# High and low parts of the attention's q and k split at the projection, not at each head's operands

## The chip, the cores and the metric

One core of a Trainium2 chip runs the kernel. The metric is the device time of one execution in microseconds, as the median of several runs. The core has five engines that work side by side, each taking its own queue of instructions in order: TensorE (PE, with its weight loads as PEld), VectorE (DVE), ScalarE (ACT), GpSimd (POOL) and SyncE (SP), which here issues every transfer (DMA).

## The reference

One decoder layer over 2048 tokens of width 1024, in float32. The embedding is normalised and modulated by a vector c; one projection `h @ w_in` gives two groups of eight heads of 64 channels each and a gate. Group A is a recurrence (RWKV-7); group B is causal attention with a bias from running forget gates:

```
proj = h @ w_in                                   # (2048, 4232)
q_f, k_f, v_f = ...                               # three slices of 512 columns, 8 heads of 64
logit[t, s] = q_t . k_s / 8 + cum[t] - cum[s]     # cum: running sum of log sigmoid of the forget gate
y_b = softmax over s <= t of logit, times v
y = concat(y_a, y_b) * silu(gate part of proj)
out = LayerNorm(alpha * x + (1 + gate_c) * (y @ w_out))
```

## The kernel before

The tokens are worked on in two halves of 1024, each in two blocks of 512. For each half there is a stretch of the recurrence and then a stretch of attention; the projection's matmuls fill TensorE beside them, ahead of need, and the output projection with the final norm ends the kernel. All work is written as generators (streams). A driver (lines 138 to 284) keeps a model of each engine's time and emits the instruction whose stream comes first by that model, so the order in each engine's queue follows from modelled costs and from when buffers come free in the model. A program change in one stream can therefore move the instructions of others.

The large products are made in the format float32r. To keep precision the kernel splits a factor x: its high part is what a copy into that format leaves of it, its low part is x minus the high part. A product is then high times high, high times low and low times high.

The steps that the change touches:

- `ev_fox` (982 to 995) takes a 128x512 tile of q, k, v or gate (two heads, 512 tokens) out of PSUM into a part of the tile `arena` (18 parts of 128x512, handed out by `slots`), stores it in DRAM (`fscr`, seen in the profile as kscr, qscr, vscr and gscr), and gives the PSUM bank back. There are 16 such tiles of q and 16 of k.
- `fox_ops` (1553 to 1582) makes four kinds of operands for each head and 512 tokens, each in a part of the tile `fx_s` (21 parts). k1 holds the high part of k in 64 rows, and three rows below: ones, and the forget sums in two parts. q1 holds the high part of q, and three rows: minus the row maximum, and two rows of ones (the first row is 0 until the maximum is known). k2 holds high k above low k, q2 low q above high q. For each, `conv` loads the raw 64x512 from DRAM into a part of `arena` (`fox_load`), ACT copies it into the operand (rounding to the high part), and for k2 POOL, for q2 DVE, subtracts that from the raw value into the other 64 rows. The three rows of k1 come by a small load from `cscr`; those of q1 are copied by DVE from the column `qrow`. Half 0 needs 64 operands (4 kinds, 2 blocks, 8 heads), half 1 needs 96, since its queries see the keys of both halves.
- `fox_guard` (1586 to 1648) multiplies q1 and k1, takes each query's largest score with DVE, and stores minus that maximum into the first of q1's three rows by a transfer (`fx_s<-mrow`). `fox_s` (1709 to 1739) waits for it, then takes for each 128 keys k1 by q1 plus k2 by q2, of which ACT makes exponentials.

In attention of half 1 DVE also prepares the output weights (`final_w`) and the rows for the final norm; those are not changed. All instructions go through one helper, so the profile gives line 134 for nearly all of them, and one has to go by tiles: `fx_s` are the attention's operands, `fx_p` its exponentials, `fx_v` its values, `rw_s` the recurrence, `ps` PSUM, `wsp` the split weights of the projection.

Of the kernel before, what the change touches and what calls it, by code (L numbers as in the profile page):

```python
# [9 lines left out]
F32 = mybir.dt.float32  # L10
# [3 lines left out]
OP = mybir.AluOpType  # L14
# [12 lines left out]
class Slots:  # L27
    """Equal parts of one tile; a part is handed out when its last use lies in the past."""
# [5 lines left out]
    def find(self, n):  # L34
        """The parts that are free first; a single one rather beside one in use, two rather at an even place."""
        best = None
        for i in self.free_:
            if all(i + j in self.free_ for j in range(n)):
                a = max(self.free_[i + j] for j in range(n))
                k = (max(a, self.drv.now), (i ^ 1) in self.free_ if n == 1 else i % 2, a)  # L40
                if best is None or k < best[0]:
                    best = (k, a, i)
        return best and best[1:]
# [20 lines left out]
class Slot:  # L64
# [14 lines left out]
    def drop(self):  # L79
        """Gives back the first part only."""  # L80
# [35 lines left out]
class Engine:  # L116
    """An engine whose instructions are also timed by the driver's model."""
# [20 lines left out]
class Driver:  # L138
    """Orders the emission. Every stream is a generator that emits a step and goes on when a model of the engines
    says that the step has ended. It yields 0 to wait for another stream, ("at", ns) to wait for a time, "pe" to  # L140
    go on as soon as the tensor engine has nothing else to do."""
# [91 lines left out]
    @contextmanager  # L233
    def side(self):
        """What is emitted here doesn't hold up its stream."""
        self.count = False
        yield
        self.count = True
# [50 lines left out]
def hymba_kernel(ctx: ExitStack, tc, x, c, emb_ln_g, emb_ln_b, w_ada, b_ada, w_in, rwkv_mix, w0,  # L289
# [50 lines left out]
    fscr = [{k: [dram.tile([128, TB], F32, name=f"{k}scr{h}{i}") for i in range(4)] for k in "qkvg"} for h in range(2)]  # L340
# [30 lines left out]
    qrow = const.tile([128, 1], F32, name="qrow")  # L371
# [48 lines left out]
    def start_loads():  # L420
        """In the order in which they are needed; the short ones between the long ones."""
# [43 lines left out]
    def start_ada(kt):  # L465
        """Shift and scale of 128 channels: four parts of the sum side by side, added up as they are transposed."""
# [30 lines left out]
    def start_lora():  # L497
        """Both low-rank factors in two parts: 0 and 1 the high part twice, 2 the low parts."""
# [22 lines left out]
    def warm():  # L521
        """Keeps the tensor engine's clock up until there is work for it."""
# [6 lines left out]
    def start_consts():  # L529
        """derived columns of pc: 0-12 one minus mix; 13-16 half a0; 17-20 half w0; 21-24 one minus k_a;  # L530
        25-32 scale, 33-40 shift of the modulated embedding"""
# [50 lines left out]
        pool.memset(qrow, 1.0)  # L582
        pool.memset(qrow[64:65], 0.0)
# [35 lines left out]
    def rsqrt(o, u, n):  # L619
        """o = u ** -0.5 on [128, n], one Newton step after the power."""  # L620
# [20 lines left out]
    def ln_group(i, xs, left):  # L641
        """Normalises some tiles of x: mean and 1/sqrt(var + eps) stay in stats."""
# [70 lines left out]
    def ln_early(b, blk, kt):  # L713
        """The first half: transposed before the factors of the modulation are known."""
# [60 lines left out]
    def plan():  # L775
        """The next 128 columns of the input projection, or tokens of the output projection."""
# [23 lines left out]
    class EarlyW:  # L800
        """More room for the first of them."""
# [7 lines left out]
    def weights():  # L809
        """Loads what the tensor engine's wide products take as the stationary operand, and splits it in two."""  # L810
# [47 lines left out]
    def proj_stream():  # L858
        """The first tiles of all go side by side, block by block; so do the last two of a half."""
# [32 lines left out]
    def shift_mix(b, g, o):  # L892
        """o = proj * (1 - mix) + previous token's proj * mix, along the free axis."""
# [17 lines left out]
    def ev_f(b, half, blk):  # L911
        """Forget gates, heads on partitions: rows of ones, and of the running sum of -8 log f in two parts."""
# [49 lines left out]
    def silu(b, g):  # L962
        """Twice the SiLU of a bank."""
# [18 lines left out]
    def ev_fox(k):  # L982
        def ev(b, half, p, blk):
            s = yield from slots.get(1)
            if k == "g":
                yield from silu(b, s)
            else:
# [3 lines left out]
            sp.dma_start(fscr[half][k][p][:, blk * NB:(blk + 1) * NB], s.ap)  # L991
# [36 lines left out]
    def bcast_rows(b, r8, w):  # L1028
        """[128 tokens, 4 tiles, n heads] -> [(head, 64 channels), 512 tokens] in a bank."""
# [7 lines left out]
    def head_sums(b, sq):  # L1037
        """Four tiles side by side, each sum 16 times, turned to [128 tokens, (4 tiles, 2 heads, 16)] in columns 128-255."""
# [13 lines left out]
    def rwkv_elem(half, p, blk, dl, u):  # L1052
        """The factors of the recurrence, decays folded in: u.kr = (kk, r), u.bk = (b, k) or (k, b) by chunk."""
# [114 lines left out]
    def rwkv_scores(u):  # L1168
        """Masked products of every chunk, the transposed factors and the right side of the solve.
        u.am: against kk; u.zs: against r, beside the transposed (b, k); u.rh: (kk, products times v) by head."""  # L1170
# [77 lines left out]
    def rwkv_solve(n, u, qt):  # L1248
        """(I + A)^-1, transposed, of every chunk and head: the two diagonal blocks, then the block between them.
        A block's rows go to 4 partitions of its quadrant, 8 rows each, beside the whole block of A."""  # L1250
# [168 lines left out]
    def rwkv_low(half, blk):  # L1419
        """Both low-rank inputs in two parts, one above the other."""  # L1420
# [28 lines left out]
    def rwkv_stream(half):  # L1449
        """All pairs of heads, both 512-token blocks of the half: unit n = 2 * pair + block."""  # L1450
# [102 lines left out]
    def fox_ops(half, st):  # L1553
        """Operands of every head: k1 = [high k; 1; -8 cum in two parts], k2 = [high k; low k],
        q1 = [high q; -row maximum; 1; 1], q2 = [low q; high q]; the maximum is 0 while it is looked for."""
        def conv(key, o, H, name, b4):
            h = H % 2
            while (b4 // 2, H // 2, name[0] + "f", b4 % 2) not in res:
                yield 0
            at = hs(1) if name == "q2" else hs(0)  # L1560
            s = yield from fox_load(name[0], H // 2, hs(h), b4 * NB, at)
            if name == "k1":
                c = (b4 % 2) * NB
                sp.dma_start(o.f[64:67], cscr[b4 // 2][:, H, c:c + NB])
            yield
            act.activation(o.ap[at], s.ap[at], AF.Copy)
            if name == "q1":
                dve.tensor_copy(o.ap[64:67], qrow[64:67, 0:1].to_broadcast([3, 512]))
            yield
            if name[1] == "2":  # L1570
                to = hs(0) if name == "q2" else hs(1)
                tt(o.ap[to], s.ap[at], o.f[at], OP.subtract, pool if name == "k2" else dve)
                yield
            s.free()
# [11 lines left out]
    def fox_guard(half, st):  # L1586
        """The row maxima of every block of queries."""
# [64 lines left out]
    def fox_exp(b, P, n0, diag):  # L1652
        """What lies after the query gets 0 once its exponential is there, whatever that is."""
# [371 lines left out]
```

## Time and profile before

| what | us |
|---|---|
| median of 3 runs | 1948.76 |
| lowest and highest run | 1947.16, 1949.63 |
| span of the profiled execution | 1952.8 |
| PE busy in it | 1805.3 (92%) |
| DVE busy | 1522.0 (78%) |
| ACT busy | 865.2 (44%) |
| POOL busy | 853.8 (44%) |

The profiled execution is one more execution, recorded by the hardware profiler; its span runs from its first to its last instruction, and no other time of it is known. "Busy" is the share of the span in which an engine executes. Matmuls are pipelined and their ends are modelled, so that a busy PE need not be PE at its peak.

### The profile page before, as it was taken

How to read it: one execution, taken by the hardware profiler on the slowest of the kernel's cores; microseconds unless marked ns; L12 is line 12 of the kernel's file. 1: busy time of each engine (PE TensorE's matmuls, PEld its weight loads, DVE VectorE, ACT ScalarE, POOL GpSimd, SP SyncE). 2: the span in 40 equal slices, each digit the busy share in tenths (PEclk: the TensorE clock that was granted, in tenths of full speed). 3: DMA queues.
4: the chain of work that ended last, by engine and by line, in shares of the span. 5: the costliest groups of instructions: out<-in, count | busy, mean ns of one | idle time of the engine just before them, and what ended most of it. 6: DMA issues, size and time to landing. Idle time of an engine off the chain costs nothing.

```text
span 1952.8 us, 31040 instructions
## 1 busy us (share of the span) xinstructions
PE 1805.3 (92%) x11049; PEld 1289.4 (66%) x11049; DVE 1522.0 (78%) x3638; ACT 865.2 (44%) x1667; POOL 853.8 (44%) x821
## 2 busy tenths in 40 slices
PE   8999989989899999999898989988999999999997
PEld 6767666767677556677676667666755554547876
DVE  5887797778863986777876887776387789887998
ACT  3464344534444665554453433533445565642000
POOL 2232341423323576733332432232247776776653
PEclk9999899999999999999998999988999999999999
DMA  9231110111113633221111111021372233213442
GB/s 286 71 104 39 49 53 23 45 47 39 55 49 114 181 113 120 81 85 57 33 58 34 49 53 39 27 60 51 111 240 69 69 97 97 88 57 103 141 134 103
DMA packets 160909, 162.24 MB, mean 83 GB/s; under 512 B 10289, under 2 KB 114306, under 8 KB 160754
## 3 DMA queue, kind: packets, MB, share of 16 engines
q1 hardware_dynamic: 160754, 160.25, 27.2%
q8 instruction: 88, 1.44, 0.3%
q14 instruction: 67, 0.55, 0.1%
HBM read 121.41 MB, written 38.73 MB: 82 GB/s over the span
## 4 chain that ended last, share of the span: by engine, by line
PE 43%; DVE 38%; issue 5%; ACT 5%; POOL 4%; DMA 3%; SPq 1%; POOLq 0%; DVEq 0%; ACTq 0%
PE ps L134 43%; DVE rw_s L134 18%; DVE arena L134 6%; DVE small L134 5%; ACT rw_s L134 4%; DVE end_s L134 2%; DVE fx_p L134 2%; DVE state L134 1%; DVE fx_s L134 1%; POOL wsp L134 1%; DVE ps L134 1%; SPq L134 1%; POOL fx_p L134 1%; DMA ada_t<-in_w_ada_dram 1%; DMA arena<-vscr 1%
## 5 line engine op out<-in xcount | busy, mean ns | idle before, releaser
L134 PE MATMUL ps<-ht,wsp 128*128 128x512 f32 x3840 | 1003.3, 408 | 6.5 <-POOL wsp L134 5.5
L134 PEld LDWEIGHTS ps<-ht,wsp 128*128 128x128 f32 x3840 | 717.2, 194 | 166.5 <-issue 9.7
L134 DVE TENSOR_TENSOR rw_s<-rw_s 128x60 f32<-128x60 f32 (+24 forms) x1056 | 338.1, 324 | 43.4 <-ACT rw_s L134 16.2
L134 POOL TENSOR_TENSOR wsp<-wst,wsp 128x1024 fp32r<-128x1024 f32 x79 | 193.9, 2455 | 267.4 <-ACT wsp L134 234.0
L134 ACT ACTIVATE rw_s<-ps 64x256 f32<-64x256 f32 (+3 forms) x448 | 179.4, 416 | 277.8 <-PE ps L134 166.5
L134 PE MATMUL ps<-rw_s 32*32 32x32 f32 (+3 forms) x2816 | 210.7, 257 | 61.9 <-DVE rw_s L134 56.4
L134 PE MATMUL ps<-fx_s 67*128 67x512 f32 (+6 forms) x960 | 259.6, 388 | 7.8 <-DVE small L134 6.5
L134 PEld LDWEIGHTS ps<-rw_s 32*32 32x32 f32 (+3 forms) x2816 | 183.5, 165 | 104.2 <-issue 47.2
L134 PEld LDWEIGHTS ps<-fx_s 67*128 67x128 f32 (+1 forms) x960 | 163.6, 191 | 124.0 <-issue 51.7
L134 ACT ACTIVATE fx_p<-ps 128x512 f32<-128x512 f32 (+3 forms) x336 | 161.6, 518 | 149.4 <-PE ps L134 126.2
L134 POOL TENSOR_TENSOR fx_p<-fx_p 128x512 f32<-128x512 f32 (+2 forms) x160 | 188.0, 1181 | 80.3 <-PE ps L134 72.6
L134 POOL TENSOR_TENSOR small<-small,nhalf 128x8 f32<-128x8 f32 (+1 forms) x48 | 71.8, 1500 | 284.9 <-DVE small L134 205.8
L134 PE MATMUL ps<-fx_p,fx_v 128*64 128x512 f32 (+3 forms) x640 | 158.7, 554 | 1.8 <-POOL fx_p L134 1.8
L134 DVE TENSOR_REDUCE small<-ps 128x1 f32<-128x512 f32 (+1 forms) x208 | 134.6, 680 | 25.0 <-PE ps L134 24.4
L134 DVE TENSOR_TENSOR fx_p<-fx_p 128x512 f32<-128x512 f32 (+1 forms) x128 | 116.2, 908 | 43.0 <-POOL fx_p L134 40.4
L134 ACT ACTIVATE wsp<-wst 128x1024 fp32r<-128x1024 f32 x80 | 84.3, 1053 | 135.3 <-DMA wst<-yscr 101.7
L134 ACT ACTIVATE arena<-ps 128x512 f32<-128x512 f32 (+2 forms) x130 | 74.8, 578 | 148.4 <-PE ps L134 143.1
L134 POOL TENSOR_TENSOR rw_s<-rw_s,arena 128x512 f32<-128x512 f32 x64 | 83.9, 1314 | 126.5 <-ACT arena L134 74.6
L134 ACT ACTIVATE fx_s<-arena 64x512 fp32r<-64x512 f32 x160 | 96.3, 624 | 13.1 <-DMA arena<-qscr 7.7
L134 DVE TENSOR_SCALAR state<-ps,dl 64x64 f32<-64x64 f32 x256 | 72.3, 282 | 29.2 <-PE ps L134 23.1
L134 DVE STREAM_TRANSPOSE rw_s<-rw_s 32x256 f32<-32x256 f32 (+1 forms) x112 | 61.7, 551 | 40.9 <-ACT rw_s L134 38.3
L134 ACT ACTIVATE rw_s<-rw_s 32x256 f32<-32x256 f32 (+1 forms) x144 | 83.3, 600 | 16.6 <-DVE rw_s L134 15.2
(151 smaller groups left out, 2067.7 us busy)
## 6 DMA issues: line engine op xcount, KB each, us to landing
wst<-in_w_in_dram SPq DMA_DIRECT2D x66, 512.0 KB
arena<-kscr SPq DMA_DIRECT2D x96, 128.0 KB
ada_t<-in_w_ada_dram SPq DMA_DIRECT2D x16, 512.0 KB
rw_l<-lowscr SPq DMA_DIRECT2D x32, 256.0 KB
arena<-qscr SPq DMA_DIRECT2D x64, 128.0 KB
arena<-in_x_dram SPq DMA_DIRECT2D x16, 512.0 KB
wst<-yscr SPq DMA_DIRECT2D x16, 512.0 KB
xe<-in_x_dram SPq DMA_DIRECT2D x8, 512.0 KB
```

The costliest lines, as they stand in the source:

```text
L134: return fn(*args, **kw)
```

## The change

DRAM keeps two tiles for each tile of q and k, its two parts, in the order in which the second operand wants them: high above low for k, low above high for q. `ev_fox` makes both: the ACT copy out of PSUM rounds to the high part, and DVE subtracts it from the PSUM bank for the low part; each is stored by a transfer of its own. `conv` in `fox_ops` then only issues transfers into the operand: two of 64 rows for k2 and q2, one of 64 rows and one of three rows for k1 and q1. The three rows of q1 (0, 1, 1) are stored in DRAM (`qscr1`) once at the start. The copies, subtractions and the staging in `arena` fall away, and `qrow` with them. Texts that only describe functions are also taken out.

```
-    fscr = [{k: [dram.tile([128, TB], F32, name=f"{k}scr{h}{i}") for i in range(4)] for k in "qkvg"} for h in range(2)]
+    fscr = [{k: [dram.tile([2, 128, TB] if k in "qk" else [128, TB], F32, name=f"{k}scr{h}{i}") for i in range(4)]
+             for k in "qkvg"} for h in range(2)]
+    qscr1 = dram.tile([3, 512], F32, name="qscr1")
...
-        pool.memset(qrow, 1.0)
-        pool.memset(qrow[64:65], 0.0)
+        qr = yield from slots.get()
+        pool.memset(qr.ap[0:3], 1.0)
+        pool.memset(qr.ap[0:1], 0.0)
+        sp.dma_start(qscr1, qr.ap[0:3])
+        qr.free()
...
     def ev_fox(k):
         def ev(b, half, p, blk):
             s = yield from slots.get(1)
+            to = fscr[half][k][p]
+            cols = slice(blk * NB, (blk + 1) * NB)
             if k == "g":
                 yield from silu(b, s)
-            else:
+            elif k == "v":
                 act.activation(s.ap, b.ap, AF.Copy)
                 b.free()
                 yield
-            sp.dma_start(fscr[half][k][p][:, blk * NB:(blk + 1) * NB], s.ap)
+            else:
+                l = yield from slots.get(1)
+                act.activation(s.r, b.ap, AF.Copy)
+                yield
+                tt(l.r, b.ap, s.ap, OP.subtract)
+                b.free()
+                i = int(k == "q")
+                sp.dma_start(to[i, :, cols], s.ap)
+                yield
+                sp.dma_start(to[1 - i, :, cols], l.ap)
+                l.free()
+            if k in "vg":
+                sp.dma_start(to[:, cols], s.ap)
             s.free()
             yield
             res[half, p, k + "f", blk] = True
...
         def conv(key, o, H, name, b4):
-            h = H % 2
             while (b4 // 2, H // 2, name[0] + "f", b4 % 2) not in res:
                 yield 0
-            at = hs(1) if name == "q2" else hs(0)
-            s = yield from fox_load(name[0], H // 2, hs(h), b4 * NB, at)
-            if name == "k1":
-                c = (b4 % 2) * NB
-                sp.dma_start(o.f[64:67], cscr[b4 // 2][:, H, c:c + NB])
-            yield
-            act.activation(o.ap[at], s.ap[at], AF.Copy)
-            if name == "q1":
-                dve.tensor_copy(o.ap[64:67], qrow[64:67, 0:1].to_broadcast([3, 512]))
-            yield
+            src = fscr[b4 // 2][name[0]][H // 2]
+            c = (b4 % 2) * NB
             if name[1] == "2":
-                to = hs(0) if name == "q2" else hs(1)
-                tt(o.ap[to], s.ap[at], o.f[at], OP.subtract, pool if name == "k2" else dve)
-                yield
-            s.free()
+                for i in range(2):
+                    sp.dma_start(o.f[hs(i)], src[i, hs(H % 2), c:c + NB])
+            else:
+                sp.dma_start(o.f[0:64], src[int(name == "q1"), hs(H % 2), c:c + NB])
+                sp.dma_start(o.f[64:67], cscr[b4 // 2][:, H, c:c + NB] if name == "k1" else qscr1)
+            yield
             st["ops"][key] = o
```

## Rows read from the trace of the kernel before

**Rows 1.** Busy us (count) by stage: PE, PEld, DVE, ACT, POOL; clock, DMA, GB/s.
```profile
130.00:615.00 485.00, 444.43 (x3312) 339.34 (x3312) 371.74 (x1117) 212.12 (x422) 156.13 (x162) 0.94 0.16 47
615.00:835.00 220.00, 210.40 (x1134) 137.88 (x1133) 168.47 (x347) 133.82 (x271) 146.99 (x168) 1.00 0.43 131
835.00:1395.00 560.00, 504.69 (x3565) 388.03 (x3565) 411.94 (x1175) 239.94 (x462) 174.25 (x171) 0.93 0.17 49
1395.00:1780.00 385.00, 373.40 (x1684) 209.76 (x1682) 310.80 (x519) 205.74 (x410) 254.83 (x237) 0.99 0.34 104
1780.00:1952.80 172.80, 157.20 (x683) 128.40 (x682) 160.16 (x237) 13.82 (x13) 87.77 (x44) 0.97 0.38 128
```

**Rows 2.** Chain of waits by line: 130-615, 640-835, 835-1395, 1425-1600, 1600-1780 us.
```profile
by line: PE ps L134 40.8%; DVE rw_s L134 34.1%; ACT rw_s L134 8.7%; DVE arena L134 4.3%; issue 3.6%; DVE small L134 3.0%; DVE state L134 2.6%; POOL small L134 1.2%; ACT arena L134 0.5%; POOL wsp L134 0.5%; POOL rw_s L134 0.4%; DVE car L134 
...
by line: PE ps L134 55.3%; DVE small L134 7.3%; POOL fx_p L134 5.8%; DVE ps L134 5.2%; DVE fx_s L134 4.3%; DVE fx_p L134 4.3%; issue 3.7%; DVE arena L134 3.6%; POOL wsp L134 2.4%; DMA arena<-vscr 2.1%; ACT arena L134 1.7%; ACT ht L134 1.0%;
...
by line: PE ps L134 44.5%; DVE rw_s L134 33.3%; ACT rw_s L134 5.1%; DVE arena L134 4.8%; issue 4.3%; DVE small L134 3.4%; DVE state L134 2.0%; ACT arena L134 0.7%; POOL rw_s L134 0.5%; POOL wsp L134 0.4%; DVE car L134 0.3%; POOL rw_l L134 0
...
by line: PE ps L134 94.7%; DVE small L134 1.1%; issue 1.1%; POOL fx_s L134 1.0%; DVE fx_p L134 0.9%; DVE fx_s L134 0.4%; DVE arena L134 0.4%; ACT fx_p L134 0.3%; POOL fx_p L134 0.2%; POOLq L134 0.0%
...
by line: PE ps L134 31.0%; DVE small L134 16.2%; DVE fx_p L134 12.2%; issue 10.0%; DVE arena L134 7.9%; DVE fx_s L134 5.6%; DVE ps L134 4.8%; POOL fx_p L134 3.7%; DVE ht L134 3.5%; POOL arena L134 2.0%; DMA arena<-kscr 1.3%; POOL fx_s L134 
```

**Rows 3.** Groups by shape, whole trace: busy us, mean ns, idle before.
```profile
L134 ACT ACTIVATE fx_s<-arena 64x512 fp32r<-64x512 f32 x160 | 96.3, 624 | 13.1 <-DMA arena<-qscr 7.7 <-DMA arena<-kscr 3.9
...
L134 DVE TENSOR_TENSOR fx_p<-fx_p 128x512 f32<-128x512 f32 x96 | 94.1, 980 | 40.9 <-POOL fx_p L134 38.8 <-ACT fx_p L134 1.1
...
L134 POOL TENSOR_TENSOR fx_s<-arena,fx_s 64x512 fp32r<-64x512 f32 x48 | 70.9, 1486 | 23.5 <-ACT fx_s L134 18.2 <-issue 2.0 <-POOL fx_p L134 1.1
...
L134 DVE TENSOR_TENSOR fx_s<-arena,fx_s 64x512 fp32r<-64x512 f32 x32 | 31.5, 994 | 0.7
...
L134 DVE CAST fx_s<-qrow 3x512 fp32r<-3x512 f32 x32 | 28.8, 916 | 0.7
...
L134 DVE TENSOR_TENSOR arena<-ps,arena 128x512 f32<-128x512 f32 x32 | 21.8, 682 | 1.0 <-PE ps L134 0.7
```

**Rows 4.** Busy time by stretch, instructions on tile fx_s alone; columns as rows 1.
```profile
615.00:835.00 220.00, 70.89 (x288) 47.91 (x288) 27.29 (x32) 38.47 (x64) 24.26 (x16) 1.00 0.43 131
1395.00:1600.00 205.00, 100.15 (x365) 62.74 (x365) 19.41 (x20) 36.31 (x61) 28.38 (x19) 1.00 0.40 124
1600.00:1780.00 180.00, 88.58 (x309) 52.94 (x307) 13.59 (x12) 21.47 (x36) 18.28 (x13) 0.98 0.27 81
```

**Rows 5.** Busy time of the late part of attention 1; columns as rows 1.
```profile
1600.00:1780.00 180.00, 171.88 (x768) 91.39 (x766) 156.81 (x249) 93.65 (x185) 132.27 (x121) 0.98 0.27 81
```

**Rows 6.** Issues on SyncE's queue, ns min/median/max: whole; recurrence 0; recurrence 1.
```profile
L134 SPq DMA_DIRECT2D arena<-kscr x96: 444/458/1427, 621.6 to 1722.9; - x96
L134 SPq DMA_DIRECT2D kscr<-arena x16: 320/332/383, 118.9 to 1423.7; - x16
...
L134 SPq DMA_DIRECT2D qscr<-arena x6: 319/324/345, 141.6 to 603.2; - x6
...
L134 SPq DMA_DIRECT2D kscr<-arena x6: 320/329/383, 902.7 to 1348.1; - x6
```

**Rows 7.** Timeline from 1614 us, VectorE and GpSimd: start, length.
```profile
1614.17 0.67 DVE L134 TENSOR_TENSOR fx_p<-fx_p 128x512 f32<-128x512 f32 x1
...
1614.85 1.27 POOL L134 TENSOR_TENSOR fx_s<-arena,fx_s 64x512 fp32r<-64x512 f32 x1 [1.01 <-issue]
1614.88 1.79 DVE L134 TENSOR_TENSOR fx_s<-arena,fx_s 64x512 fp32r<-64x512 f32 x1
```

**Rows 8.** Costliest groups of the page, GpSimd.
```profile
L134 POOL TENSOR_TENSOR fx_p<-fx_p 128x512 f32<-128x512 f32 (+2 forms) x160 | 188.0, 1181 | 80.3 <-PE ps L134 72.6
```

**Rows 9.** Waits of SyncE's queue in attention 1: us, times, longest.
```profile
SPq L134 <- ACT mrow L134: 42.3, 11, 11.6
...
SPq L134 <- PE ps L134: 12.7, 13, 2.8
```

More of the change, by code (lines that the diff above doesn't have):

```diff
@@ L370, in hymba_kernel @@
     wf = const.tile([128, KT, 8], F32, name="wf")
-    qrow = const.tile([128, 1], F32, name="qrow")
     state = const.tile([128, 2, 4, 2, 64], F32, name="state")
@@ L1556, in conv @@
         def conv(key, o, H, name, b4):
-            h = H % 2
             while (b4 // 2, H // 2, name[0] + "f", b4 % 2) not in res:
                 yield 0
-            at = hs(1) if name == "q2" else hs(0)
-            s = yield from fox_load(name[0], H // 2, hs(h), b4 * NB, at)
-            if name == "k1":
-                c = (b4 % 2) * NB
-                sp.dma_start(o.f[64:67], cscr[b4 // 2][:, H, c:c + NB])
-            yield
-            act.activation(o.ap[at], s.ap[at], AF.Copy)
-            if name == "q1":
-                dve.tensor_copy(o.ap[64:67], qrow[64:67, 0:1].to_broadcast([3, 512]))
-            yield
-            if name[1] == "2":
-                to = hs(0) if name == "q2" else hs(1)
-                tt(o.ap[to], s.ap[at], o.f[at], OP.subtract, pool if name == "k2" else dve)
-                yield
-            s.free()
+            src = fscr[b4 // 2][name[0]][H // 2]
+            c = (b4 % 2) * NB
+            if name[1] == "2":
+                for i in range(2):
[3 more added lines that the diff above has]
+                sp.dma_start(o.f[64:67], cscr[b4 // 2][:, H, c:c + NB] if name == "k1" else qscr1)
+            yield
             st["ops"][key] = o
```

## The prediction

> **What bounds the kernel now.** An average over unlike stages decides nothing, so I first cut the span where the work changes, with the view of busy time by stretch [rows 1]: recurrence of half 0 (130 to 615 us), attention of half 0 (615 to 835), recurrence of half 1 (835 to 1395), attention of half 1 (1395 to 1780) and the tail. TensorE (PE) is 90 to 92% busy in the recurrences and 96 to 97% in the attention stages; VectorE (DVE) is at 74 to 81%, and at 93% in the tail. ScalarE (ACT) and GpSimd (POOL), from which the change takes most work, are at 53 to 67% even in the attention stages.
>
> Then I read the chain of waits stage by stage, to see which engine sets the end [rows 2]. In the recurrences it is 41 to 45% PE and 44% DVE (its lines rw_s, arena, small and state added up). In attention 0 it is 55% PE and 25% DVE. Attention 1 has two regimes: until 1600 us 95% PE, from then on only 31% PE and some 50% DVE. ACT has no line over 2% in any attention stretch. So what the change takes from ACT buys almost nothing by itself, and what it does to DVE counts in every stretch but one.
>
> **What it removes.** 160 ACT copies into the operands (96.3 us), 48 POOL subtractions for k2 (70.9), 32 DVE subtractions for q2 (31.5) and 32 DVE copies of three constant rows (28.8) [rows 3]. All lie in the attention stages; the DVE part is 27.3 us in attention 0, 19.4 until 1600 and 13.6 from 1600 to 1780 [rows 4].
>
> How much of that lies on the path? The chain's line "DVE fx_s" is just these two DVE instructions.
> - 1600 to 1780: 5.6% of 180 us [rows 2], 10.1 us of the 13.6 busy. The bounds are 0 and 13.6; I take 10, since DVE leads the chain there.
> - 1425 to 1600: DVE fx_s 0.4% and POOL fx_s 1.0% of 175 us [rows 2], 2.5 us. The bounds are 0 and 19.4; I take 2.5, since PE holds 95% of the chain.
> - 640 to 835: 4.3% of 195 us [rows 2], 8.4 us. But PE idles only 220.0 - 210.4 = 9.6 us in that stage [rows 1], and the projection matmuls that fill it must be done some time anyway. The bounds are 0 and 9.6; I take 7.
>
> Gains: 10 + 2.5 + 7 = 19.5 us.
>
> PE's busy share needs a second look, for 171.9 us busy of 180 would leave only 8 to gain after 1600. The weight loads fill 91 us of those 180, against 339 of 485 in recurrence 0 [rows 1, 5]. Per microsecond PE gets less done there than elsewhere although it is "busy": its matmuls stand waiting inside their recorded times. So the chain is my measure, and 10 us may pass the 8.
> *The Trainium skill (Perfetto Trace Analysis, Identifying the Most-Contended Engine) says that matmul busy time is no measure of headroom and that the busy share of the weight loads is. By the first the late stretch could give 8 us, by the second all 13.6 of its DVE time. The trace agrees with the second, in that the two shares part ways where the chain leaves PE.*
>
> **What it adds.** Each of the 32 tiles of q and k that leave the projection takes one more DVE subtraction, 128x512, one input in PSUM. The nearest row has the same shape and kinds of operands: 682 ns [rows 3], so 21.8 us of DVE in all. By the stores to DRAM, ten of the 32 fall into recurrence 0 and twelve into recurrence 1 [rows 6] (the rows show the six of q in recurrence 0, beside which there are four of k, and the six of k in recurrence 1, beside six of q), two come before 130 us and eight in the attention stages. An instruction put into DVE's queue costs as much as DVE's time is on the path there. In recurrence 0, DVE has 44.0% of the chain and is busy 371.7 of 485.0 us, 76.6% [rows 1, 2], so 57%; in recurrence 1 it is 43.5% against 73.6%, 59%. Hence 10 x 0.682 x 0.57 = 3.9 and 12 x 0.682 x 0.59 = 4.8 us. The two early ones add 1. For the eight in attention, 24.7% against 76.6% makes 32%: 8 x 0.682 x 0.32 = 1.8. Costs: 11.5 us; bounds 0 (all in DVE's gaps) and 21.8 (all on the path).
>
> **What it moves.** The ACT copy out of PSUM stays, and only rounds its output. The bank goes back after the subtraction, 0.68 us and a hand-over later. With eight banks I put that at 0; if PE stood for the bank each time it would be 32 x 0.68 = 22 us. A second part of the arena is held meanwhile, while 160 short holdings of it go: 0. The row of constants is stored once, beside the start's transfers; under 1 us if not hidden.
>
> Transfers: 160 loads of 128 KB and 48 of 6 KB become 240 and 80, and 32 stores come on top. A load takes 0.45 us of SP's queue, a store 0.33 [rows 6]: in attention 0, 16 rows of constants and 32 second halves are 48 issues, 22 us; in attention 1, 16 and 48 are 64, 29 us. The DMA engines are 43% and 34% busy there [rows 1]; that is no limit. What counts is the order. SP takes its queue in turn, and a load now goes straight into the operand's tile: SP itself waits for the last matmul that read the tile, where before the load went to the arena and the ACT copy did that waiting. Behind it stand the stores of the row maxima, which fox_s waits for, and the weight loads. Against that, an operand needs no copy (0.62 us) and no subtraction (0.99 or 1.49 us at the mean [rows 3]) after it has landed. I put the two together at 0; the price if the queue binds is the third rival's.
>
> **Sum.** -19.5 + 11.5 = -8 us. The profiled span is 1952.8 us, and the median of the runs, 1948.8, lies 4 below it; a term of 8 us is the same against either. So 1948.8 - 8 = 1941 us.
>
> **The rivals.**
> 1. *More: POOL lets go of DVE.* A q2 subtraction took 1.79 us while POOL's k2 subtraction ran beside it; a sum of two SBUF tiles, twice as many partitions and the same length, had taken DVE 0.67 just before, alone [rows 7]. Those sums have a mean of 980 ns over 96 [rows 3]: 96 x (0.98 - 0.67) = 30 us of stretch. POOL's two-input work in attention is 188.0 us on fx_p [rows 8] and 70.9 on fx_s; without the latter, 27%, about 8 us of stretch should go. With all the DVE time after 1600 (13.6 instead of 10) and half the costs: 19.5 + 3.6 + 8 - 6 = 25 us less, 1924. Against it: part of the stretch lies before 1600, where PE leads. *The Trainium skill (SBUF — State Buffer, Who interferes with whom) has POOL and DVE share a pair of ports that one instruction locks whole when DVE reads two tiles of SBUF; with one input in PSUM DVE doesn't contend. The trace agrees with the first half: 1.79 against 0.67 us. By that rule the added subtractions stay at 682 ns.*
> 2. *No change.* PE's work is untouched. If PE's busy share binds after all, the attention stages give back a third of the 9.6 and 8.1 us that PE idles, 6 us, and half of the costs takes it away: 1949.
> 3. *Slower: SP's queue binds in attention 1.* SP waits there 42.3 us for the row maxima and 12.7 for PE [rows 9]. The 12.7 stand beside 32 loads of constants that go straight into operands; with all 96 operands loaded so they would be 38, 25 more. With the 29 us of issues SP's queue grows by 54 us. Much of it can replace waits for work that isn't due. If half lies ahead of a row maximum or an operand that PE then wants, 27 us: 1941 + 27 = 1968. It makes the kernel slower than before from 8 of the 54 us on. Against it: SP is seldom named in the chain in the attention stretches, and an operand is asked for a head ahead.
>
> **How the numbers follow.** Forecast (1933 to 1945): 0.42. Rival 1 (1915 to 1933): 0.19. Rival 2 (1945 to 1953): 0.18. Rival 3 (1953 to 1968): 0.21. A change under 0.2%, 4 us, is about what a measurement of this kernel can't tell. So faster is 0.61, same 0.18, slower 0.21. The likeliest case's own range is 1933 to 1945. The range for 8 in 10 must reach into both signs: 1920 leaves out the far end of rival 1 and 1959 that of rival 3, one in ten each.
>
> **What would show it.** Right: no ACT, POOL or DVE instruction writes fx_s any more; DVE's busy time falls by some 38 us (60.3 less 21.8), ACT's by 96, POOL's by 71; attention 1 is some 12 us shorter, attention 0 some 5 to 7, each recurrence 4 to 5 longer. For rival 1, DVE's mean for sums of fx_p falls well below 980 ns. For rival 3, SP's waits for PE in attention 1 pass 38 us, and PE waits for loads of fx_s. What would make it wrong in either direction: the order of all instructions is written by a model of the engines, which now sees other costs, so any stage may be reordered by several microseconds for reasons in none of these terms.

## The result and the profile after

The changed kernel takes 1915.32 us (median of 4 runs, 1910.95 to 1920.98) against 1947.96 for the kernel before beside it (4 runs). The ratio is 0.9831, with a 95% interval of 0.9803 to 0.9859: 33 us faster, where 8 were forecast and 1920 to 1959 was the range. The profiled execution fell from a span of 1952.8 us to 1912.4.

The page of the changed kernel: the engines' busy time, and the chain that ended last by engine.
```profile
span 1912.4 us, 30878 instructions
...
PE 1786.4 (93%) x11049; PEld 1278.3 (67%) x11049; DVE 1474.0 (77%) x3606; ACT 781.2 (41%) x1507; POOL 777.3 (41%) x773
...
PE 45%; DVE 37%; ACT 6%; issue 4%; DMA 4%; POOL 3%; SPq 2%; POOLq 0%; DVEq 0%; ACTq 0%
```
Against the table of before, ACT has lost 84 us of busy time, POOL 76.5 and DVE 48. That is mostly the work that the change takes out, and PE has the same 11049 matmuls.

Groups by shape, to be read beside [rows 3]: busy us, mean ns of one, idle before.
```profile
L134 DVE TENSOR_TENSOR fx_p<-fx_p 128x512 f32<-128x512 f32 x96 | 87.3, 909 | 58.0 <-POOL fx_p L134 57.5
...
L134 DVE TENSOR_TENSOR arena<-ps,arena 128x512 fp32r<-128x512 f32 x32 | 22.0, 686 | 38.5 <-ACT arena L134 38.3
```
The added subtraction costs 686 ns, as its neighbour in [rows 3] did (682). The sums of fx_p fell from 980 to 909 ns.

The stages, cut where [rows 1] cut them, at the last store of each half's recurrence or attention: recurrence 0, attention 0, the norm and recurrence 1, attention 1, tail.
```profile
131.00:619.00 488.00, 450.48 (x3376) 345.37 (x3377) 378.60 (x1130) 216.34 (x428) 158.28 (x162) 0.97 0.18 55
619.00:814.00 195.00, 192.46 (x1060) 123.75 (x1059) 139.00 (x312) 93.33 (x199) 112.54 (x146) 1.00 0.54 165
814.00:1363.00 549.00, 507.14 (x3627) 390.42 (x3626) 419.59 (x1196) 246.00 (x469) 176.92 (x176) 0.97 0.20 59
1363.00:1739.00 376.00, 361.63 (x1627) 202.07 (x1626) 274.48 (x480) 152.64 (x312) 208.31 (x205) 0.97 0.39 123
1739.00:1912.40 173.40, 159.55 (x700) 130.81 (x698) 160.95 (x246) 13.84 (x13) 85.90 (x43) 0.98 0.39 132
```
The clock column stands out: 0.97 in both recurrences, where [rows 1] have 0.94 and 0.93. The trace holds each stretch in which TensorE was granted half speed (1.2 instead of 2.4 GHz). Half of their length is a first estimate of what they cost. With the projection's matmuls (128x512, 0.256 us of PE's time each: 981.3 us by 3840) counted in every stage, the two profiles compare so:

| stage | us before, after | lost at half speed | projection matmuls |
|---|---|---|---|
| start | 128.1, 131.4 | 5.1, 3.4 | 201, 207 |
| recurrence 0 | 488.2, 487.2 | 27.3, 17.1 | 1053, 1091 |
| attention 0 | 214.0, 195.7 | 0, 0 | 313, 269 |
| norm of half 1 | 48.0, 53.6 | 0, 0 | 179, 212 |
| recurrence 1 | 518.0, 494.6 | 39.3, 17.1 | 1107, 1106 |
| attention 1 | 386.6, 376.1 | 3.4, 10.2 | 320, 255 |
| tail | 169.9, 173.8 | 4.5, 3.8 | 667, 700 |

Of the 40.4 us between the two profiles, 28.0 are half speed. Without it and with every projection matmul charged where it runs, the rest is -12.4 us: attention and norm -10.6, recurrences -1.4, start +3.5, tail -3.8. In what follows, "full-clock time" is the span times the mean granted clock, taken for every run: 1873.5 us before (median of 73 runs) and 1859.3 after. It treats the whole span as if it went by TensorE's clock. Among those 73 runs 0.010 of clock goes with 15.6 us where the product counts 20, so it makes the clock's share somewhat too large.

### The profile page after: what moved, and what is told of

The parts are those of the page before. It is cut to its first block, busy times and chain, and to the rows that moved or that the text cites. A ratio compares the mean times of both kernels' runs of the same rounds, so it can differ in the third digit from the quotient of the medians.

```text
span 1912.4 us, 30878 instructions
## 1 busy us (share of the span) xinstructions
PE 1786.4 (93%) x11049; PEld 1278.3 (67%) x11049; DVE 1474.0 (77%) x3606; ACT 781.2 (41%) x1507; POOL 777.3 (41%) x773
## 4 chain that ended last, share of the span: by engine, by line
PE 45%; DVE 37%; ACT 6%; issue 4%; DMA 4%; POOL 3%; SPq 2%; POOLq 0%; DVEq 0%; ACTq 0%
PE ps L134 45%; DVE rw_s L134 19%; DVE arena L134 8%; ACT rw_s L134 4%; DVE small L134 4%; DVE end_s L134 3%; SPq L134 2%; DVE state L134 2%; DVE fx_p L134 1%; DMA wst<-in_w_in_dram 1%; DVE ht L134 1%; POOL wsp L134 1%; ACT arena L134 1%; POOL small L134 1%; DMA arena<-vscr 1%
## 5 line engine op out<-in xcount | busy, mean ns | idle before, releaser
L134 PE MATMUL ps<-ht,wsp 128*128 128x512 f32 x3840 | 981.3, 403 | 4.2 <-POOL wsp L134 3.5
L134 PEld LDWEIGHTS ps<-ht,wsp 128*128 128x128 f32 x3840 | 707.5, 191 | 161.0 <-issue 10.0
L134 ACT ACTIVATE rw_s<-ps 64x256 f32<-64x256 f32 (+2 forms) x448 | 181.7, 418 | 264.4 <-PE ps L134 134.0
L134 PE MATMUL ps<-fx_s 67*128 67x512 f32 (+5 forms) x960 | 257.5, 390 | 4.4 <-ACT mrow L134 2.3
L134 PEld LDWEIGHTS ps<-rw_s 32*32 32x32 f32 (+3 forms) x2816 | 179.4, 161 | 95.5 <-issue 55.9
L134 DVE TENSOR_TENSOR fx_p<-fx_p 128x512 f32<-128x512 f32 (+1 forms) x128 | 111.5, 871 | 64.1 <-POOL fx_p L134 62.2
L134 ACT ACTIVATE arena<-ps 128x512 f32<-128x512 f32 (+3 forms) x130 | 75.0, 579 | 174.1 <-PE ps L134 169.8
L134 ACT ACTIVATE wsp<-wst 128x1024 fp32r<-128x1024 f32 x80 | 84.2, 1053 | 143.0 <-PE ps L134 69.6
L134 DVE TENSOR_TENSOR arena<-ps,arena 128x512 fp32r<-128x512 f32 (+4 forms) x108 | 73.2, 678 | 43.7 <-ACT arena L134 40.7
L134 ACT ACTIVATE rw_s<-rw_s 32x256 f32<-32x256 f32 (+1 forms) x144 | 83.4, 601 | 19.2 <-DVE rw_s L134 17.7
```

The source lines that it names most:

```text
L134: return fn(*args, **kw)
```

## The experiments

The theories after the result were these. *Work*: the gain is the removed work, in the attention stages. *Order*: the gain comes from the new order of all instructions, which the kernel's model of the engines writes out anew when any cost changes, and through it from TensorE's clock. What each expects is in the words recorded before every run.

### Old order with the light work, new order with the heavy work

e1 keeps the order of before on every engine. The 160 ACT copies, 80 subtractions and 32 constant rows are counted in the order but not issued; transfers go straight into the operands. The low parts are zero and q and k stay whole at the projection.
```
-            act.activation(o.ap[at], s.ap[at], AF.Copy)
+            drv.time(act, "activation", [o.ap[at], s.ap[at]], {})
```


> The kernel before with its order of instructions on every engine, but the heads' copies and subtractions are left out and transfers go straight into the operands (the low parts are zeros, so the output lacks them; the split at the projection is not made). Theory A (the work taken off the engines acts where it lay, whatever the order): about 1948 - 20 = 1928, attention 0 some 7 to 12 us shorter, attention 1 some 12, recurrence 1 unchanged. Theory B (the rewritten order and the faster clock that goes with it carry most): 1940 to 1948.

e2 keeps the changed kernel's order and adds stand-ins for all the removed work, written into unused rows of the operands and unknown to the model.
```
+            nc.scalar.activation(dst, src_, AF.Copy)
+            if name == "q1":
+                nc.vector.tensor_copy(t.ap[96:99], nhalf[96:99, 0:1].to_broadcast([3, 512]))
+            if name == "q2":
+                nc.vector.tensor_tensor(dst, src_, src_, op=OP.subtract)
+            if name == "k2":
+                nc.gpsimd.tensor_tensor(dst, src_, src_, op=OP.subtract)
```


> The changed kernel with its order, and beside it dummies of the removed work at the same points: 160 ACT copies, 32 DVE subtractions and 32 DVE row copies, 48 POOL subtractions, which nothing waits for. Theory A: it gives back about 20 us or more, 1935 to 1942, all of it in the attention stages. Theory B: it gives back under 10 us, 1915 to 1925, and recurrence 1 stays at 495 us.

Measured: e1 1945.06 us, ratio 0.9987 (0.9952 to 1.0021); e2 2001.28, 1.0272 (1.0203 to 1.034). At full clock e1 is 1861, 12 less than before, and its clock is 0.958 against 0.963, so that nearly all of it is lost again. The 12 us lie in the attention stages (-4 and -8 by the reckoning of the table above), and half speed takes 11.8 us more in the profile (91.4 for 79.6). In time e1 came out as theory B had it. e2 misses both figures, and goes theory A's way much further than A had it: work that the order does not know costs 31 us in attention 0 and 57 in attention 1, of which 12 and 27 are half speed by the same first estimate. Recurrence 1, which holds none of the removed work, is the clean part. Busy time in it, for before, after, e1 and e2 (columns as [rows 1]):
```profile
878.30:1396.30 518.00, 466.36 (x3390) 357.92 (x3391) 379.60 (x1118) 216.53 (x428) 159.98 (x163) 0.92 0.16 47
```
```profile
867.90:1362.50 494.60, 454.39 (x3390) 348.57 (x3390) 383.28 (x1131) 217.54 (x429) 159.84 (x163) 0.97 0.18 54
```
```profile
879.90:1403.70 523.80, 470.23 (x3390) 360.64 (x3391) 381.61 (x1118) 216.87 (x428) 160.26 (x163) 0.92 0.16 46
```
```profile
900.80:1398.40 497.60, 458.53 (x3390) 351.63 (x3390) 380.19 (x1131) 217.25 (x429) 159.62 (x163) 0.96 0.18 53
```
All four do the same 3390 matmuls. The length goes with the order (518 and 524, 495 and 498), not with the work. So the 23 us of recurrence 1 are the order's, and 22 of them are half speed (39.3 less 17.1).

### The added subtractions alone

e3 is the kernel before, with its order, plus the 32 VectorE subtractions behind the projection and 32 more stores, all unknown to the model.
```
                 act.activation(s.ap, b.ap, AF.Copy)
+                if k in "qk":
+                    nc.vector.tensor_tensor(b.ap, b.ap, s.ap, op=OP.subtract)
+                    nc.sync.dma_start(xscr, s.ap)
                 b.free()
```


> The kernel before in its order, with the 32 added DVE subtractions (into the bank itself, result unused) and 32 added stores where q and k leave the projection. The forecast's cost: 11.5 us, 1959, with 4 to 5 us in each recurrence. If DVE's gaps hide them: 1948 to 1951.

Measured 1976.46 us, ratio 1.0161 (1.0099 to 1.0223), at full clock 17 us more, and over both figures. But not where the prediction has it: recurrence 0 is 7 us shorter and recurrence 1 7 us longer, while attention 1, with four of the 32, is 20 us longer (386.6 to 407.1). In recurrence 0 and attention 1 most of this is the clock: with half speed taken off, recurrence 0 changes by +0.1, recurrence 1 by +5.1 and attention 1 by +3.2. The extra stores lie in the same places, so this run doesn't tell the two apart.

### The same kernels in other orders

One constant of the model is changed and nothing else: ACT's latency from 165 to 180 ns (e4 on before, e5 on after), the cost of an issue on SP from 600 to 640 (e7, e6), DVE's latency from 130 to 145 (e11, e8), PE's from 197 to 212 (e14, e15). As an example:
```
-LATENCY = dict(pe=197.0, act=165.0, dve=130.0, pool=100.0, sp=0.0)
+LATENCY = dict(pe=197.0, act=180.0, dve=130.0, pool=100.0, sp=0.0)
```


> The kernel before, only the model's latency of ACT set from 165 to 180 ns: the same work in another order. Theory A: within 0.3% of before (1942 to 1954). Theory B, where the order alone moves the time by about a per cent: anything between 1925 and 1970, and the recurrences change by 10 us or more at equal counts of PE instructions, with the granted clock moving along.

> The changed kernel, the model's latency of ACT set from 165 to 180 ns, as in the earlier run of the kernel before that came to 1970. If the change is worth some 33 us whatever the order, about 1970 - 33 = 1937. If its order was a lucky draw and the change itself is worth the forecast's 8 us, about 1962. Recurrence 1 back at 505 to 520 us with a granted clock of 0.92 to 0.94 would say that its 23 us are the order's.

> The changed kernel, the model's cost of an issue on SP set from 600 to 640 ns. Same reading against its pair, the kernel before with the same model: 33 us apart if the change is worth that in any order, 8 if only the forecast's, with the sign open if luck decides.

> The kernel before, the model's cost of an issue on SP set from 600 to 640 ns: the pair of the run above. By luck of the order alone 1935 to 1975.

> The changed kernel, the model's latency of DVE set from 130 to 145 ns. A third draw of the order: within 10 us of 1915 if the order counts little once the work is gone, 1925 to 1950 if 1915 was a good draw.

> The kernel before, its order written with the model's latency of VectorE at 145 instead of 130 ns: the partner of the changed kernel under the same model (1956). Theory A (the change is worth 12 to 15 us of full-clock time in any order, and the clock is the order's): full-clock time 1870 to 1882 against 1862; the time itself 1945 to 1985, on either side of 1956, since the clock may fall anywhere from 0.95 to 0.965. Rival (the change itself raises the clock): clock under 0.954 and over 1968.

> The kernel before, its order written with the model's latency of TensorE at 212 instead of 197 ns. Theory A (the change is worth 14 to 32 us of full-clock time in any order, the clock is drawn with the order): full-clock time 1873 to 1895 and clock 0.953 to 0.968, 1940 to 1985. Rival (the 33 us are the draw of these two orders alone): the two kernels of this model within 8 us of each other at full clock.

> The changed kernel under the same model as the run before (TensorE's latency 212 ns). Theory A: full-clock time 1856 to 1863 again, as in the four orders so far, clock 0.953 to 0.973, so 1912 to 1955. Rival: full-clock time over 1868, within 8 us of its partner.

Medians, before and after under the same model:

| model | us | full-clock time | clock | ratio to before as it is (95%) |
|---|---|---|---|---|
| as it is | 1948, 1915 | 1873.5, 1859.3 | 0.962, 0.973 | 1, 0.9831 (0.9803 to 0.9859) |
| ACT latency | 1970, 1931 | 1880, 1860 | 0.957, 0.964 | 1.0115 (1.0057 to 1.0172), 0.9932 (0.99 to 0.9965) |
| SP issue cost | 1952, 1943 | 1877, 1861 | 0.963, 0.958 | 1.0025 (0.9997 to 1.0052), 0.9976 (0.9947 to 1.0006) |
| DVE latency | 1984, 1956 | 1894, 1862 | 0.956, 0.954 | 1.0173 (1.0145 to 1.02), 1.004 (1.0005 to 1.0076) |
| PE latency | 1921, 1911 | 1866, 1846 | 0.972, 0.966 | 0.9844 (0.9797 to 0.9891), 0.9796 (0.9748 to 0.9843) |

The kernel before spreads over 63 us with its work untouched, and one of its orders (1921) has most of the gain of the change. The differences are -33, -39, -9, -28 and -10 us: mean -24, 95% interval over five pairs -41 to -7. At full clock they are -14, -20, -16, -32 and -20: mean -20, -29 to -12, and the changed kernel is below its partner each time. Its full-clock time hardly moves with the order except in the last (1859 to 1862, then 1846, so the forecast for e15 of 1856 to 1863 was missed downward). The clock averages 0.962 before and 0.963 after: over these five pairs it comes with the order and is no property of the change. Three runs miss both of their forecasts: e8's 1956 is more than 10 us from 1915 and over the 1950 of a good draw, e11 has a time that both allow, but a clock of 0.956 and the highest full-clock time of these ten, and e14 is faster in time, clock and full-clock time than either theory had it. The rival of that pair, two kernels within 8 us at full clock, falls with its 20.

### One part of the change at a time

e12 splits only q at the projection, e13 only k; the other goes the old way. e16 and e17 are the same two under DVE's latency of 145 ns.
```
-            elif k == "v":
+            elif k in "vk":
...
+        conv = lambda key, o, H, name, b4: (conv_new if name[0] == "q" else conv_old)(key, o, H, name, b4)
```


> Only q is split where the projection leaves PSUM; k goes the old way. Removed: the 32 VectorE subtractions for q2, the 32 VectorE copies of constant rows, 64 of the 160 ScalarE copies; added: 16 VectorE subtractions; GpSimd's 48 subtractions for k2 stay. Theory A (the gain at full clock is VectorE's own removed work): full-clock time 1860 to 1867, nearly all of the 12 to 15. Rival (it comes from GpSimd letting go of VectorE): 1869 to 1876. The time itself depends on the clock that the new order gets: 1910 to 1960 by either.

> Only k is split where the projection leaves PSUM; q goes the old way. Removed: GpSimd's 48 subtractions for k2 and 96 of the 160 ScalarE copies; added: 16 VectorE subtractions (11 us); the 32 VectorE subtractions for q2 and the 32 copies of constant rows stay. Theory A (the gain at full clock is VectorE's own removed work, which is q's alone): full-clock time (span by mean clock) 1870 to 1890, no gain over before's 1873. Rival (GpSimd's and ScalarE's share pays too): 1855 to 1866. The time itself depends on the clock of the new order: 1935 to 1985 by A, 1915 to 1950 by the rival.

> Only q split at the projection, under the model's order with VectorE's latency at 145 ns, where before stands at 1984 (full-clock time 1894) and the whole change at 1956 (1862). Theory A (q alone is the gain): full-clock time 1855 to 1868. Rival (k has a part in it): 1872 to 1890.

> Only k split at the projection, the order written with VectorE's latency at 145 ns, where full-clock time is 1894 before, 1862 with the whole change and 1862 with q alone. Theory A (the gain is q's, that is VectorE's own removed work; k's 1859 in the first order was the draw): 1878 to 1895. Rival (either part brings the whole gain): 1855 to 1868. In between, k has half.

The ratios to before are 0.9887 (0.9866 to 0.9909), 0.9868 (0.9806 to 0.993), 0.9939 (0.991 to 0.9967) and 1.0075 (1.0042 to 1.0109).

| | neither | q | k | both |
|---|---|---|---|---|
| us | 1948 | 1926 | 1928 | 1915 |
| full-clock time | 1873.5 | 1857 | 1859 | 1859 |
| us, DVE latency 145 | 1984 | 1936 | 1963 | 1956 |
| full-clock time | 1894 | 1862 | 1871 | 1862 |

q alone has the whole gain at full clock in both orders, as theory A said. But k alone has it too in the first order and 23 of 32 us in the other, though it leaves DVE's 60 us in place and adds 16 subtractions. So for the whole kernel theory A falls, and the totals of the parts don't add up. The stages tell more. Against the kernel before of the same model, with half speed and projection matmuls taken off as above (one profile each):

| change in us | q | k | both |
|---|---|---|---|
| attention 0 | -10.3 | -0.8 | -7.0 |
| attention 1 | -5.3 | -7.3 | -0.8 |
| both recurrences | -4.5 | -9.7 | -1.4 |
| attention 0, DVE latency 145 | -8.9 | -1.5 | -8.2 |
| attention 1, DVE latency 145 | -7.6 | -9.9 | -17.7 |
| both recurrences, DVE latency 145 | -12.1 | -11.5 | -13.5 |

In attention 0 the gain is q's, that is DVE's own work, in both orders (in e12, 23 small matmuls of that stage ran elsewhere, some 3 us). Much of k's total lies in the recurrences, which hold none of the removed work. In attention 1 k does have a part.

The DVE sums of fx_p in e12 and in e1:
```profile
L134 DVE TENSOR_TENSOR fx_p<-fx_p 128x512 f32<-128x512 f32 x96 | 95.4, 994 | 47.1 <-POOL fx_p L134 44.1 <-ACT fx_p L134 2.2
```
```profile
L134 DVE TENSOR_TENSOR fx_p<-fx_p 128x512 f32<-128x512 f32 x96 | 86.2, 898 | 42.4 <-POOL fx_p L134 41.5
```
They take 994 ns where POOL still makes k2 (e12), 898 and 909 where it doesn't (e1, after). That is the release of rival 1, 7 us of DVE's time. e12 has the full gain without it, so the gain doesn't need it; whether it has a part in what k alone wins in attention 1 is open.

### Filling TensorE's idle time

What lowers the clock? In before's trace, around 1160 us (columns as [rows 1]):
```profile
1152.00:1156.00 4.00, 4.00 (x19) 3.34 (x18) 3.76 (x9) 0.16 (x1) 2.67 (x3) 1.00 0.19 70
1156.00:1160.00 4.00, 2.24 (x10) 1.51 (x9) 3.98 (x7) 1.63 (x2) 1.37 (x1) 1.00 0.00 0
1160.00:1164.00 4.00, 0.00 (x0) 0.00 (x0) 3.88 (x9) 0.00 (x0) 0.98 (x1) 0.78 0.47 120
1164.00:1168.00 4.00, 2.95 (x48) 2.74 (x48) 3.90 (x10) 0.72 (x1) 1.27 (x1) 0.50 0.04 11
1168.00:1172.00 4.00, 4.00 (x45) 2.85 (x39) 0.55 (x2) 1.38 (x3) 2.08 (x4) 0.50 0.00 0
1172.00:1176.00 4.00, 4.00 (x13) 3.42 (x14) 0.00 (x0) 1.02 (x3) 0.37 (x2) 0.52 0.02 4
1176.00:1180.00 4.00, 4.00 (x41) 3.67 (x40) 2.59 (x8) 3.02 (x7) 0.92 (x4) 1.00 0.00 0
```
PE stands idle for 6.8 us, waiting for DVE; the clock falls while it waits, and the work behind runs at 0.50 for some 11 us more. All half-speed stretches of the recurrences, in the traces of before and after, begin in or just behind such an idle, of 1.1 us or more. The reverse doesn't hold: in before, 14 idles of 1.0 to 1.6 us in the recurrences have no half speed right behind them, and in after one of 2.8 us (at 893 us) has none. *The Trainium skill (TensorE: Matmul & The Clock Gate, HAM oscillation — how this bites in real kernels) describes this: PE re-throttles while it waits (there for a DMA), and it reckons the cost as half of the throttled time. The trace agrees on the first; on the second see below.* PE's longest group of waits from 130 to 1390 us, us in total, times, longest, for before and for after:
```profile
PE ps L134 <- DVE rw_s L134: 61.3, 30, 6.8
```
```profile
PE ps L134 <- DVE rw_s L134: 53.8, 36, 4.5
```
After the change this group has more waits, and shorter ones. The longest wait alone doesn't foretell the clock, though: e14 has one of 7.1 us (46.8 us in all) and a clock of 0.972. The test puts matmuls of the identity, overwritten by what follows, ahead of those calls at which PE had idled 1 us or more, in the given order: 135 in before (e9; its words say 17 calls, the edit has 16), 113 in after (e10), 96 in the PE-latency order of after (e18).
```
+    fillers = {"scores": {1: 5, 3: 12, 5: 4, 8: 6, 9: 7, 10: 7, 13: 17}, "solve": {1: 7, 3: 3, 5: 3, 6: 13, 9: 6, 10: 9, 13: 9, 14: 12, 15: 15}}
+    def fill(kind, b):
+        for _ in range(fillers[kind].get(calls[kind], 0)):
+            nc.tensor.matmul(b.ap[:, 0:128], ident, ident, start=True, stop=True, skip_group_check=True)
+        calls[kind] += 1
```


> The kernel before, in its own order, with 135 extra matmuls of the identity by itself (0.28 us each by the rows of the start, 37 us in all; their result is overwritten by the matmul behind them) ahead of the 17 calls of the recurrences' scores and solve at which TensorE had stood idle for 1.0 to 6.8 us waiting for VectorE; each call gets some 70% of its idle. Theory A (TensorE's granted clock falls where the engine has stood idle, and most of the 33 us came from fewer and shorter idles of this kind, since the order changed): the half-speed stretches behind those idles, 116 of the 161 us of half speed, mostly go; the granted clock rises from 0.96 to 0.975 or more, and the median falls to 1890 to 1920, though TensorE does more; full-clock time (span by mean clock) stays at 1870 to 1890. Theory B (the clock follows the load, the chip or chance, not these idles): clock 0.955 to 0.965, and the fillers cost 0 to 37 us: 1950 to 1985.

> The changed kernel with 113 such extra matmuls (32 us) ahead of its own 18 calls with idles of 1.0 us or more. Theory A: of the 105 us at half speed some 60 lie behind these idles and mostly go; clock 0.98 or more, full-clock time 1858 to 1875, median 1885 to 1900. Theory B: clock 0.965 to 0.975, 1912 to 1945.

> The changed kernel in the order of the model with TensorE's latency 212 ns (1911, clock 0.966, full-clock time 1846), with 96 identity matmuls (27 us) ahead of the 15 calls of scores and solve at which TensorE had stood idle 1.0 us or more there. Theory A (idles lower the clock, fillers cost half of what they take): clock 0.975 to 0.982, full-clock time 1855 to 1866, median 1892 to 1910. Theory B (fillers buy nothing): clock below 0.971 or median 1911 or more.

The same place in e9, where 17 fillers precede the wait:
```profile
1152.00:1156.00 4.00, 4.00 (x28) 3.61 (x27) 3.95 (x9) 1.64 (x2) 1.26 (x1) 1.00 0.00 0
1156.00:1160.00 4.00, 2.15 (x20) 1.95 (x18) 3.91 (x7) 0.00 (x0) 1.11 (x1) 1.00 0.41 109
1160.00:1164.00 4.00, 3.08 (x50) 2.72 (x51) 3.90 (x11) 1.29 (x3) 1.27 (x1) 0.71 0.09 27
1164.00:1168.00 4.00, 4.00 (x40) 2.90 (x39) 0.41 (x2) 1.54 (x4) 2.46 (x5) 0.50 0.00 0
1168.00:1172.00 4.00, 4.00 (x15) 3.29 (x16) 0.00 (x0) 0.96 (x4) 0.00 (x0) 0.51 0.00 0
1172.00:1176.00 4.00, 4.00 (x43) 3.63 (x43) 2.90 (x9) 2.77 (x6) 1.19 (x4) 1.00 0.02 4
```
The idle is 4.0 us shorter (2.8 left), the half-speed stretch 3.4 (10.2 us instead of 13.7). Over the runs the clock rises from 0.962 to 0.977 and the time falls to 1939.84 us, ratio 0.9942 (0.9913 to 0.9971), though PE is given 34 us more work. That idle time makes the clock fall is thus shown: the fillers are all that was added, in an order that is otherwise before's. That half speed costs half of the throttled time is not borne out: this loss in the profile falls by 34.5 us (79.6 to 45.1), the time by only 10, the full-clock time rises by 20, and theory A's 1890 to 1920 is missed. Either the fillers were partly in the way or PE was not the limit in all of the slow stretches; the runs don't tell which. On after, e10 raises the clock to 0.978 and gains nothing: 1914.61 us, ratio 0.9823 (0.9806 to 0.984), a time as in theory B with a clock that neither theory had. e18 came out as its theory A had it and has the lowest median of all: 1902.68 us, ratio 0.9759 (0.97 to 0.9818). It is 9 below its order without fillers, but that one ran on another chip and the intervals of the two ratios overlap.

## Why the prediction was wrong

**The failed step is the last one of its text: the order's own effect stood at nothing in the sum.** The prediction added terms at a fixed order and named the reordering only as what could make it wrong, by several microseconds in a stage. In place of that, other orders moved the unchanged kernel between 1921 and 1984 us. With the change, the drawn order gave TensorE 0.973 instead of 0.962 of its clock: 1859.3 us at 0.962 would be 1933, at 0.973 it is 1911. Some 20 of the 33 us are this (17 by the 15.6 us per 0.010 of the 73 runs), all of it in the recurrences, which hold none of the removed work; e1, with the light work in the old order, stayed at 1945. The sign could not be known: in two of the other four models the changed kernel has the lower clock by 0.005 or more. The size could have been bounded: [rows 1] show 0.94 and 0.93 there, and 6 to 7% below full speed in 1045 us is a term of tens of microseconds that any reordering can move.

**A second step is not borne out: the cost in the recurrences.** 8.7 us (3.9 and 4.8) were charged to the subtractions by DVE's share of the chain. Over the five pairs the recurrences change by -1.9 us, once half speed and projection matmuls are taken off (95% interval -12 to +8, single pairs -13.5 to +7.9); in before's own order e3 has +5.2 there, with its stores. So a cost of a few microseconds is not excluded, and one of 8.7 is unlikely. The subtractions took 686 ns where 682 were forecast, and DVE idles 38 us before them waiting for ACT's copy, a wait that the prediction had left out.

**The gains were of the right size, and in one stage for the reason given.** 19.5 less 1.8 were forecast for the attention stages. Over the five pairs they give -20.0 us by the same reckoning, the norm included; in the order on hand -10.6. In attention 0 the five pairs lie close together, -7.0 to -9.6 (mean -8.7), where 7 were forecast as DVE's own work; q alone, which takes that work away, has this gain and k alone has not. There DVE's share of the chain was a good price. In attention 1 the mean of -13.5 is near the 12.5 forecast, but the pairs scatter from -0.8 to -27.8, and k alone gains there though DVE's work stays: the size was right, the reason isn't shown. What q's and k's part share (their ACT copies, the landings in `arena`, SP's order) was not taken apart further. The raw figures are not to be compared with the forecast of each stage: attention 0 fell by 18.3 us, of which 44 projection matmuls that ran elsewhere are 11. One reading behind the gains was too quick: that the busy shares of PE and of its weight loads part ways where the chain leaves PE. By [rows 1] and [rows 5] they are 98% and 58% from 1395 to 1600 us too, where PE has 95% of the chain.

**The rest.** Busy time fell by 84, 76.5 and 48 us where 96, 71 and 38 were forecast. The bank at 0 stands: PE and its weight loads waited 9.8 us in all for DVE's work on arena before and 8.1 after. Of the rivals, the first comes nearest in time (1924), and its 8 us of release were 7, but the gain doesn't need them. The second falls: in the five pairs the change gained at full clock each time. The third has its sign and, in some orders, its effect. SyncE's waits in attention 1, beside [rows 9]:
```profile
SPq L134 <- PE ps L134: 71.0, 32, 10.5
SPq L134 <- ACT mrow L134: 56.6, 12, 10.9
```
SP waits 71.0 us for PE, far over the 38 named, and the stage is 10.5 us shorter all the same. The chain of the whole stage (1363 to 1739 us):
```profile
by line: PE ps L134 65.0%; SPq L134 6.8%; DVE fx_p L134 4.3%; issue 3.8%; DVE arena L134 2.6%; DVE small L134 2.4%; POOL fx_p L134 2.3%; DMA arena<-in_b_ada_dram 2.1%; DVE ht L134 1.9%; DMA fx_s<-qscr 1.7%; DMA arena<-vscr 1.5%; DMA arena<-
```
SP's queue has 25.5 us of it, 21 of them before 1396 us, and the landing of an operand of q 6.3; before the change SP has 0.8 and no operand lands on the chain. In the five pairs SP and such landings have some 31 us of this chain after the change in two (as it is, and PE latency) and under 1 us in three. By the reckoning above attention 1 gains 0.8 and 5.2 us in the two, 27.8, 16.2 and 17.7 in the three. That is what the third rival describes, beside a larger gain than was forecast; no run takes SP's queue by itself, so it is not shown to be the cause. The late part of the stage (1560 to 1739 us), beside the last line of [rows 2]:
```profile
by line: PE ps L134 67.3%; DVE fx_p L134 4.8%; DVE arena L134 4.7%; issue 4.5%; DVE ht L134 4.0%; DMA arena<-vscr 3.2%; DVE small L134 2.8%; POOL fx_p L134 2.4%; POOL wsp L134 1.3%; POOL arena L134 1.3%; ACT fx_p L134 1.3%; DVE ps L134 0.7%
```
SP has 0.2% of it: here SP's waits were for operands that nobody wanted yet. PE now leads where DVE did (67% for 31%).

## What to carry to other kernels

Where a planner writes the order, time one change under several of its models before a few per cent are put down to the change: here the draw alone moved the unchanged kernel by 63 us, and the change is worth some 24 on average (7 to 41), not the 33 of one pair. Compare span times granted clock as well as time: it was steadier here, though it counts the clock somewhat too high. Then compare stage by stage: the total put q and k on a level, and attention 0 told them apart. Behind an idle of TensorE look for half speed; filling such idles raised the clock in all three orders tried, and the time gained by it was 10 us, nothing, and 9 that noise may hide.

## What the runs showed of the hardware

The same program on the same chip has no fixed clock: 27 runs of the kernel before on one chip had 0.955 to 0.968 and took 1939 to 1960 us. 73 runs on four chips took 1936 to 1966 us at 0.953 to 0.970, with a correlation of -0.92 between time and clock, while span times clock stayed within 1868 to 1882. Half speed often lasted longer than the idle that it followed: in before's trace an idle of 1.3 us near 338 us stands ahead of 10 us at half speed. It can be shorter too: in after's trace an idle of 4.5 us near 1261 us stands ahead of 3.4 us.
